# Two plain blocks ahead of the first feed-forward stage's doubles in an encoder layer on one NeuronCore, one double more, and another order of the operand combinations

## The chip, the cores and the metric

The kernel runs on one core of one Trainium2 chip. The metric is the time of one execution of the program on the device, in microseconds (us). A time given for a kernel is the median of its runs.

## What is computed

One layer of a bidirectional encoder with 512 tokens, 1024 features and float32 numbers. It adds half a SwiGLU feed-forward stage to x, then a mixer (a dilated local attention A, a grouped-query attention B with rotary embeddings, gates, an output projection), then half a second feed-forward stage, and normalises the result:

```python
def swiglu(x, w1, w3, w2):
    return (jax.nn.silu(x @ w1) * (x @ w3)) @ w2
...
    for l in range(DEPTH):
        x = x + 0.5 * swiglu(rmsnorm(x, ffn1_norm[l]), ffn1_w1[l], ffn1_w3[l], ffn1_w2[l])
        h = rmsnorm(x, mix_norm[l])
        x = x + hybrid_mixer(h, w_in[l], b_gate[l], q_norm[l], k_norm[l], rel_bias,
                             w_branch_a[l], w_branch_b[l], w_out[l], cos, sin)
        x = x + 0.5 * swiglu(rmsnorm(x, ffn2_norm[l]), ffn2_w1[l], ffn2_w3[l], ffn2_w2[l])
    return rmsnorm(x, final_norm)
```

`w1` and `w3` are 1024 x 2816, `w2` is 2816 x 1024. The hidden width of 2816 is 22 blocks of 128, numbered f = 0 to 21.

## The kernel before

**Arithmetic.** Each float32 operand is split into a high part that TensorE multiplies in one pass and the remainder (`H`, `L`). A product is three matmuls (`mm3`): H by H, H by L, L by H. For weights the split is a cast on ScalarE (`L234`, 128x1024) and a subtraction on VectorE (`L235`).

**Plain blocks.** The activations h lie as eight tiles of 128 features x 512 tokens (`hH0` to `hH7`, `hL0` to `hL7`). A plain block f takes one weight chunk of `w1` and one of `w3` (128x1024 each). Each chunk makes 8 steps of three matmuls with 512 columns in a PSUM bank of its own. The first block does both chunks together (`pair`), the others one after the other (`feat`). The loop over the plain blocks counts these steps: n = 0 to 63 with four blocks. After a step it calls hooks: at n = 12 the squares for the norm, at 23 the statistic (`stat_r`), at 28 its spreading over the partitions (`stat_R`, which gives `R`, the reciprocal norm of each token). The bank of a chunk can't be emptied before `R` is there, so these evictions are held and then issued at once (`done1`: a multiplication by `R`, `L473`, and a Silu; `done3`: `L477`). There are four such banks (`psm`, bufs=4): with four chunks held, the next product needs the bank of the first.

**Doubles.** From there on two blocks f, f+1 are done together by a seven-product scheme of Strassen's kind (`strassen`): steps A11, S1, S2, A12, S3, S4, A22, each of 8 x 3 matmuls with 256 columns. Steps S2 and S4 use weight sums that VectorE adds (`L233`). For S1 and S3 the sums are made by DMA: one load from SP's queue, and a second that adds to it from GpSimd's queue (`L215`, `L216`). The steps of following doubles are woven into each other (`slots`): A11, S1, S2, A12, then A11 of the next double, S3, S1 of the next, and so on.

**Operand combinations.** The doubles need combinations of the quarters of h. `t_steps` makes them: eight copies of the scaled x into two scratch tiles T0 and T1 (ScalarE, `L343`), four combinations on VectorE (`L356`, `L357`), and the splits of them: `part(0)` for S1, `part(3)` for S2, `part(2)` for A22 (`L348`, `L349`), and four small ones, `part1`, for S3 (`L353`, `L354`). The plain loop calls one of the first fifteen at n = 16, 18, ..., 44; the four small ones are called after the first steps of the doubles.

**What sets the order of the work.** TensorE's program order is the order of the code (`manual_schedule`). A scheduler orders the instructions of ScalarE, VectorE, GpSimd and SP's queue when the program is built; on the chip each of them runs its own list in that order. Weight chunks are used in the order of `self.order`; loads are issued in the order of `turn_of`, which puts the two-part sums (`wt`) four places earlier; every kind of buffer is a ring (`BUFS`): three raw chunks `wr`, three `wa`, two `ws`, four `wt`, and three split chunks `wh`/`wl` and one more, `whx`, which takes every fourth chunk.

**Groups.** `GROUPS` says at which f the plain blocks end and where the groups end, whose outputs go through `w2` together. In the first stage ("a") blocks 0 to 3 are plain, and 4 to 7 are two doubles; then `w2` for blocks 0 to 7, and two more groups of doubles. In the second ("b") blocks 0 and 1 are plain and 2 to 7 are three doubles.

Of the kernel before, what the change touches and what calls it, by code (L numbers as in the profile page):

```python
# [18 lines left out]
BUFS = {"wr": 3, "wa": 3, "ws": 2, "wt": 4, "wh": 3, "whx": 1}  # L19
BASE = {"wh": 160, "whx": 32}  # L20
EARLY, EARLIER = 4, 6
GROUPS = {"a": (4, 8, 16, 22), "b": (2, 8, 16, 22)}
PAIRS = ((0, 0), (1, 0), (0, 1), (0, 2), (1, 1), (1, 2), (2, 0), (3, 0), (2, 1), (2, 2), (3, 1), (3, 2))
NSQ = 10
STEPS = ("A11", "S1", "S2", "A12", "S3", "S4", "A22")
# [9 lines left out]
T = 512  # L35
# [34 lines left out]
class Layer:  # L70
    def __init__(self, ctx, tc, a):
        self.tc, self.nc, self.a = tc, tc.nc, a
        ctx.enter_context(tc.manual_schedule(engines={mybir.EngineType.PE}))
        pool = lambda n, **k: ctx.enter_context(tc.tile_pool(name=n, **k))
# [38 lines left out]
        self.raws, self.tiles, self.used, self.wx, self.TQ = {}, [], 0, None, None  # L113
# [46 lines left out]
    def ring(self, tag, n, done, last):  # L160
        held, bufs = self.rings[tag], BUFS[tag]
        pool = self.wb if tag in ("wr", "wh") else self.wx
        if pool is None or (len(held) >= bufs and held[-bufs] >= done):
            return None
        held.append(last)
        if tag[:2] != "wh":
            return pool.tile([128, 1024], F32, tag=tag, name=tag, bufs=bufs)
        at = (self.offset(n) - BASE[tag]) % 256 // 4
        return tuple(pool.tile([128, 1088], F32R, tag=t, name=t, bufs=bufs)[:, at:at + 1024] for t in ("wh", "wl"))
# [164 lines left out]
    def t_steps(self, g, gp):  # L334
        nc = self.nc
        raw, both = [], []
        flat = lambda t, c: t[:, c].rearrange("p k n -> p (k n)")

        def put(d):
            if d == 0:  # L340
                both.extend(gp.tile([128, 2048], F32, tag=f"g{2 + c}", name=f"T{c}") for c in range(2))
                raw.extend(both[c // 2][:, 1024 * (c % 2):1024 * (c % 2) + 1024] for c in range(4))
            nc.scalar.activation(both[d // 4].rearrange("p (a c) -> p a c", a=2)[:, :, 256 * (d % 4):256 * (d % 4) + 256],  # L343
                                 self.x[d].rearrange("p (a n) -> p a n", a=2), AF.Copy, scale=self.par[:, g + d:g + d + 1])

        def part(c):
            src, H, L = raw[c], flat(self.TH, max(0, c - 1)), flat(self.TL, max(0, c - 1))
            nc.scalar.copy(H, src)  # L348
            nc.vector.tensor_sub(L, src, f32(H))  # L349

        def part1(k):
            src, H, L = raw[1][:, 256 * k:256 * k + 256], self.hH[k][:, 256:512], self.hL[k][:, 256:512]
            nc.scalar.copy(H, src)  # L353
            nc.vector.tensor_sub(L, src, f32(H))  # L354

        sub = lambda o, a, b: nc.vector.tensor_sub(raw[o], raw[a], raw[b])  # L356
        neg = lambda o, a, b: nc.vector.scalar_tensor_tensor(raw[o], raw[a], -1.0, raw[b], op0=ALU.mult, op1=ALU.subtract)  # L357
        return ([lambda d=d: put(d) for d in range(NK)]
                + [lambda: sub(0, 0, 1), lambda: sub(1, 3, 1), lambda: neg(3, 3, 0), lambda: part(0),
                   lambda: neg(2, 3, 2), lambda: part(3), lambda: part(2)], [lambda k=k: part1(k) for k in range(4)])  # L360

    def block(self, name, n):
        if n % 8 == 0:
# [71 lines left out]
    def ffn(self, s, gin, gnext, hooks, out=None, side=None):  # L435
        with ExitStack() as ctx:
            pool = lambda n, **k: ctx.enter_context(self.tc.tile_pool(name=n, reuse_waits="tile", **k))
            tp = pool("hT", bufs=1, side="right")
            self.TH = tp.tile([128, 3, 4, 256], F32R, name="TH")
            self.TL = tp.tile([128, 3, 4, 256], F32R, name="TL")  # L440
            self.wx = self.shifted(pool("wx", bufs=1), 128)
            self.cp = self.shifted(pool("c", bufs=2), 128)
            self.ffn_run(s, gin, gnext, hooks, out, side or {}, pool("g", bufs=1))
            self.wx = None

    def ffn_run(self, s, gin, gnext, hooks, out, side, gp):
# [83 lines left out]

        first, *ends = GROUPS[s]

# [206 lines left out]
    def project_qk(self):  # L739
        nc, tc = self.nc, self.tc  # L740
        with ExitStack() as ctx:
            pool = lambda n, **k: ctx.enter_context(tc.tile_pool(name=n, reuse_waits="tile", **k))
            tp = self.shifted(pool("qT", bufs=1), 64)
            self.TQ = [tp.tile([128, 4, 4, 256], F32R, name=f"TQ{c}") for c in "HL"]
            self.wx = self.shifted(pool("wxq", bufs=1), 64)
# [440 lines left out]
    def layer(self, out):  # L1186
# [7 lines left out]
        for d in range(NK):  # L1194
            nc.sync.dma_start(self.x[d], self.a["x"][d])
            if d % 2 == 0:
                s = slice(128 * d, 128 * d + 256)
# [121 lines left out]
```

## Time and profile before

| | |
|---|---|
| time before, median of 3 runs | 1253.38 us (1253.02 to 1253.86) |
| the profiled execution's own time | 1252.48 us |
| its span, first to last instruction | 1250.7 us |
| mean granted TensorE clock | 0.998 |
| TensorE busy | 1239.0 us, 99% of the span |
| VectorE busy | 891.4 us, 71% |
| ScalarE busy | 595.6 us, 48% |
| moved by DMA | 183.49 MB, mean 147 GB/s |

The profile is of one execution. Times in its timeline are microseconds from the start of the span. PE is TensorE, DVE is VectorE, ACT is ScalarE, POOL is GpSimd; SPq and POOLq are the queues that issue DMAs. A row of the timeline gives start, duration, engine, line, operation, output<-input, shapes and, in brackets, how long the engine sat idle before it and what ended that. Durations of matmuls overlap (they are pipelined), so a matmul's price is the distance from its start to the next one's start. On DVE and ACT, too, an operation starts a little before the one ahead of it has ended.

### The profile page before, as it was taken

The page shows a single profiled execution, that of the slowest core. Times are in us where ns is not written, and L with a number is a line of the kernel's source. Part 1 is how long each engine was busy: PE and PEld are TensorE (multiplying, and loading weights), DVE is VectorE, ACT ScalarE, POOL GpSimd, SP SyncE. Part 2 cuts the span into 40 slices and gives each one's busy share as a digit, 9 for nine tenths or more (in the row PEclk, how much of TensorE's full clock was granted, in tenths as well). Part 3 has the DMA queues.
Part 4 walks back from the last instruction along what each step waited for, and adds up shares of the span by engine and source line. Part 5 has one row for each costly group of instructions (what it writes and reads, how often), then busy time and mean ns, then how long its engine had stood idle before and what let it go on. Part 6 is the DMA issues. An engine that isn't in the chain of part 4 may idle for free.

```text
span 1250.7 us, 20135 instructions
## 1 busy us (share of the span) xinstructions
PE 1239.0 (99%) x8076; PEld 1112.9 (89%) x8076; DVE 891.4 (71%) x1344; ACT 595.6 (48%) x886; POOL 122.6 (10%) x128
## 2 busy tenths in 40 slices
PE   9999999999999999999999999999999999999997
PEld 7897999899898999978888878888889989988997
DVE  7784688468784887567745898866678747874874
ACT  8551365245463444454423546654475425532553
POOL 1111101000210210200000200000301001100001
PEclk9999999999999999999999999999999999999999
DMA  9875777241486882762242220157737536743222
GB/s 299 229 193 166 194 194 197 87 119 55 148 209 190 226 236 87 228 186 78 84 141 88 81 93 18 34 155 233 218 101 189 166 101 185 187 151 107 63 85 68
DMA packets 85981, 183.49 MB, mean 147 GB/s; under 512 B 12528, under 2 KB 19072, under 8 KB 85888
## 3 DMA queue, kind: packets, MB, share of 16 engines
q1 hardware_dynamic: 68048, 141.27, 33.7%
q0 software_dynamic: 17120, 40.39, 16.1%
q8 instruction: 63, 1.03, 0.3%
q10 hardware_dynamic: 720, 0.55, 0.1%
q14 instruction: 30, 0.25, 0.1%
HBM read 170.55 MB, written 15.29 MB: 149 GB/s over the span
## 4 chain that ended last, share of the span: by engine, by line
PE 97%; DVE 1%; ACT 1%; DMA 0%; issue 0%; SPq 0%; POOL 0%; DVEq 0%
PE mm L249 25%; PE mm L251 24%; PE mm L250 24%; PE Y L250 4%; PE Y L249 4%; PE Y L251 4%; PE X L250 2%; PE X L251 2%; PE X L249 2%; PE mm L937 1%; PE S L861 1%; PE Tb L1073 1%; PE T L948 1%; PE Sb L251 1%; PE Sb L250 1%; PE Sb L249 1%
## 5 line engine op out<-in xcount | busy, mean ns | idle before, releaser
L234 ACT CAST wh<-wr 128x1024 fp32r<-128x1024 f32 x139 | 145.9, 1049 | 194.7 <-PE mm L250 125.7
L235 DVE TENSOR_TENSOR wl<-wr,wh 128x1024 fp32r<-128x1024 f32 x139 | 169.6, 1221 | 51.5 <-ACT wh L234 51.2
L249 PE MATMUL mm<-hH,wh 128*128 128x256 f32 (+1 forms) x600 | 198.2, 330 | 0.0
L251 PE MATMUL mm<-hH,wl 128*128 128x256 f32 (+1 forms) x600 | 195.4, 326 | 1.0 <-DVE wl L235 1.0
L250 PE MATMUL mm<-hL,wh 128*128 128x256 f32 (+1 forms) x600 | 195.5, 326 | 0.3 <-DVE hL L389 0.3
L249 PE MATMUL mm<-gg,wh 128*128 128x512 f32 (+1 forms) x376 | 141.5, 376 | 0.0
L250 PE MATMUL mm<-gg,wh 128*128 128x512 f32 (+1 forms) x376 | 141.0, 375 | 0.0
L251 PE MATMUL mm<-gg,wl 128*128 128x512 f32 (+1 forms) x376 | 141.0, 375 | 0.0
L251 PEld LDWEIGHTS mm<-hH,wl 128*128 128x128 f32 x600 | 112.9, 188 | 11.8 <-DVE wl L235 1.4
L249 PEld LDWEIGHTS mm<-hH,wh 128*128 128x128 f32 x600 | 112.8, 188 | 11.7 <-issue 1.0
L250 PEld LDWEIGHTS mm<-hL,wh 128*128 128x128 f32 x600 | 113.0, 188 | 10.4 <-DVE hL L389 0.8
L234 ACT CAST wh<-wa 128x1024 fp32r<-128x1024 f32 x50 | 52.6, 1052 | 102.1 <-PE mm L250 55.4
L234 ACT CAST wh<-wt 128x1024 fp32r<-128x1024 f32 x50 | 52.6, 1052 | 71.1 <-PE mm L250 46.4
L235 DVE TENSOR_TENSOR wl<-wt,wh 128x1024 fp32r<-128x1024 f32 x50 | 61.2, 1224 | 33.1 <-ACT wh L234 32.4
L234 ACT CAST wh<-ws 128x1024 fp32r<-128x1024 f32 x50 | 52.6, 1052 | 66.6 <-PE mm L250 47.5
L249 PE MATMUL mm<-TH,wh 128*128 128x256 f32 x304 | 83.9, 276 | 0.0
L250 PE MATMUL mm<-TL,wh 128*128 128x256 f32 x304 | 83.9, 276 | 0.0
L251 PE MATMUL mm<-TH,wl 128*128 128x256 f32 x304 | 83.9, 276 | 0.0
L249 PEld LDWEIGHTS mm<-gg,wh 128*128 128x128 f32 x376 | 70.6, 188 | 14.1 <-PE mm L251 0.9
L251 PEld LDWEIGHTS mm<-gg,wl 128*128 128x128 f32 x376 | 70.6, 188 | 12.9
L250 PEld LDWEIGHTS mm<-gg,wh 128*128 128x128 f32 x376 | 70.6, 188 | 12.6
L545 DVE TENSOR_TENSOR u<-mm,R 128x512 f32<-128x512 f32 x40 | 27.7, 691 | 75.7 <-PE mm L251 75.5
(270 smaller groups left out, 3210.0 us busy)
## 6 DMA issues: line engine op xcount, KB each, us to landing
wr<-in_w2a SPq DMA_DIRECT2D x22, 512.0 KB, 3.4
wr<-in_w2b SPq DMA_DIRECT2D x22, 512.0 KB, 3.5
wt<-in_w13b SPq DMA_DIRECT2D x20, 512.0 KB, 3.5
wa<-in_w13b SPq DMA_DIRECT2D x20, 512.0 KB, 3.3
wt<-in_w13b POOLq DMA_DIRECT2D x20, 512.0 KB, 6.0
wt<-in_w13a SPq DMA_DIRECT2D x18, 512.0 KB, 3.5
wt<-in_w13a POOLq DMA_DIRECT2D x18, 512.0 KB, 6.1
wa<-in_w13a SPq DMA_DIRECT2D x18, 512.0 KB, 3.4
```

The source lines that it names most:

```text
L234: self.nc.scalar.copy(H, raw)
L235: self.nc.vector.tensor_sub(L, raw, f32(H))
L249: mm(out, lH, rH, start=start, stop=False, skip_group_check=more)
L250: mm(out, lH, rL, start=False, stop=False, skip_group_check=more)
L251: mm(out, lL, rH, start=False, stop=stop, skip_group_check=more)
L545: nc.vector.tensor_mul(u, ps, R)
L861: nc.tensor.matmul(*args, start=True, stop=True)
L937: nc.tensor.matmul(oc, v, p, start=st, stop=sp)
L948: nc.tensor.transpose(ps[:, 128 * b:128 * b + 128], P[h][:, c0 + 128 * b:c0 + 128 * b + 128], self.ident)
L1073: nc.tensor.transpose(pt[:, 128 * j:128 * j + 128], P[h, j][:, 128 * k:128 * k + 128], self.ident)
```

## The change

Five edits. `GROUPS["a"]` starts with 2 instead of 4: blocks 2 and 3, which were plain, become a double. The hooks of the first stage move: squares from n = 12 to 10, `stat_r` from 23 to 22, `stat_R` from 28 to 27, and the combinations from every second step from n = 16 to every step from n = 15. `t_steps` returns another list, for both feed-forward stages: `part(0)` directly behind the combination that it needs, `part(3)` next, and the combination and split for A22 (`neg(2,3,2)`, `part(2)`) moved behind the four small splits, to the calls after the first steps of the doubles. The ring gives out a buffer for a double's weights (other than split ones) only to the stage that runs.

```diff
-GROUPS = {"a": (4, 8, 16, 22), "b": (2, 8, 16, 22)}
+GROUPS = {"a": (2, 8, 16, 22), "b": (2, 8, 16, 22)}
...
-        if pool is None or (len(held) >= bufs and held[-bufs] >= done):
+        s = self.order[n][0]
+        if pool is None or s[:2] == "sw" and tag != "wh" and s[2] != self.stage or (len(held) >= bufs and held[-bufs] >= done):
             return None
...
         return ([lambda d=d: put(d) for d in range(NK)]
-                + [lambda: sub(0, 0, 1), lambda: sub(1, 3, 1), lambda: neg(3, 3, 0), lambda: part(0),
-                   lambda: neg(2, 3, 2), lambda: part(3), lambda: part(2)], [lambda k=k: part1(k) for k in range(4)])
+                + [lambda: sub(0, 0, 1), lambda: part(0), lambda: sub(1, 3, 1), lambda: neg(3, 3, 0), lambda: part(3)],
+                [lambda k=k: part1(k) for k in range(4)] + [lambda: neg(2, 3, 2), lambda: part(2)])
...
-            hooks = {12: squares, 23: self.stat_r, 28: self.stat_R, "T": (16, 2)}
+            hooks = {10: squares, 22: self.stat_r, 27: self.stat_R, "T": (15, 1)}
```

In the changed kernel all line numbers from 160 on are one higher. The scheduler orders the other engines anew; three places are shown here. In the rows `acc<-acc,sq` sums the squares, `wl` is the remainder of a weight chunk (`wl<-wr,wh` of a plain one), `ws` a weight sum, `ms` the first step from the statistic to `R`, T_316 and T_317 are T0 and T1 (T_302 and T_303 in the changed kernel), `TL` the remainder of a combination, `t_381` (`t_377`) the eviction of the first chunk's bank.

VectorE from the last sums of squares on, which is where TensorE starts the second plain block; before:

```order
L399 TENSOR_TENSOR acc<-acc,sq 128x512 x3
L235 TENSOR_TENSOR wl<-wr,wh 128x1024
L399 TENSOR_TENSOR acc<-acc,sq 128x512
L356 TENSOR_TENSOR T_316<-T_316 128x1024
L235 TENSOR_TENSOR wl<-wr,wh 128x1024 x2
L356 TENSOR_TENSOR T_316<-T_317,T_316 128x1024
```

The same place in the changed kernel:

```order
L400 TENSOR_TENSOR acc<-acc,sq 128x512 x4
L357 TENSOR_TENSOR T_302<-T_302 128x1024
L236 TENSOR_TENSOR wl<-wr,wh 128x1024 x2
L234 TENSOR_TENSOR ws<-wt,wa 128x1024
L236 TENSOR_TENSOR wl<-wa,wh 128x1024
L357 TENSOR_TENSOR T_302<-T_303,T_302 128x1024
```

The remainder of the second block's first chunk, which stood ahead of the last sum of squares, stands behind it and behind the first combination now; and a weight sum `ws<-wt,wa` stands between.

VectorE from the statistic to the first eviction; before:

```order
L405 TENSOR_SCALAR ms<-stat 128x4
L357 SCALAR_TENSOR_TENSOR T_317<-T_317,T_316 128x1024
L235 TENSOR_TENSOR wl<-wr,wh 128x1024
L349 TENSOR_TENSOR TL<-T_316,TH 128x1024
L357 SCALAR_TENSOR_TENSOR T_317<-T_317 128x1024
L473 TENSOR_TENSOR t_381<-mm,R 128x512
```

The same place in the changed kernel, from the operation behind `ms<-stat` and the first `TL` on:

```order
L358 SCALAR_TENSOR_TENSOR T_303<-T_303,T_302 128x1024
L236 TENSOR_TENSOR wl<-wt,wh 128x1024
L236 TENSOR_TENSOR wl<-wa,wh 128x1024
L350 TENSOR_TENSOR TL<-T_303,TH 128x1024
L355 TENSOR_TENSOR hL_105<-T_302,hH_97 128x256
L355 TENSOR_TENSOR hL_106<-T_302,hH_98 128x256
L355 TENSOR_TENSOR hL_107<-T_302,hH_99 128x256
L355 TENSOR_TENSOR hL_108<-T_302,hH_100 128x256
L358 SCALAR_TENSOR_TENSOR T_303<-T_303 128x1024
L234 TENSOR_TENSOR ws<-ws,wa 128x1024
L350 TENSOR_TENSOR TL<-T_303,TH 128x1024
L474 TENSOR_TENSOR t_377<-mm,R 128x512
```

Between the statistic and the first eviction stood four operations of 1024 columns; now there are eight of them (the first `TL` is not in the rows) and four of 256.

ScalarE from the last square on, at the second plain block; before:

```order
L397 ACTIVATE sq<-x_81 128x512
L234 CAST wh<-wr 128x1024
L343 ACTIVATE T_316<-x_75,par 128x2x256
L343 ACTIVATE T_316<-x_76,par 128x2x256
L343 ACTIVATE T_316<-x_77,par 128x2x256
L343 ACTIVATE T_317<-x_78,par 128x2x256
L234 CAST wh<-wr 128x1024
```

And in the changed kernel:

```order
L398 ACTIVATE sq<-x_81 128x512
L344 ACTIVATE T_302<-x_75,par 128x2x256
L344 ACTIVATE T_302<-x_76,par 128x2x256
L344 ACTIVATE T_302<-x_77,par 128x2x256
L235 CAST wh<-wr 128x1024
L344 ACTIVATE T_303<-x_78,par 128x2x256
L235 CAST wh<-wr 128x1024
```

Three copies of x into T0 stand ahead of the cast of the second block's first chunk now.

On GpSimd's list one adding load stood ahead of the operation that finishes the statistic (`r<-ms`), and three stand there now; on SP's list the first `wt` load stands one place earlier, ahead of the second block's first chunk.

More of the change, by code (lines that the diff above doesn't have):

```diff
@@ L112, in __init__ @@
         self.order += self.ffn_order("b")
-        self.raws, self.tiles, self.used, self.wx, self.TQ = {}, [], 0, None, None
+        self.raws, self.tiles, self.used, self.wx, self.TQ, self.stage = {}, [], 0, None, None, None
         self.cap = len(self.order)
@@ L440, in ffn @@
             self.TL = tp.tile([128, 3, 4, 256], F32R, name="TL")
-            self.wx = self.shifted(pool("wx", bufs=1), 128)
+            self.wx, self.stage = self.shifted(pool("wx", bufs=1), 128), s
             self.cp = self.shifted(pool("c", bufs=2), 128)
@@ L744, in project_qk @@
             self.TQ = [tp.tile([128, 4, 4, 256], F32R, name=f"TQ{c}") for c in "HL"]
-            self.wx = self.shifted(pool("wxq", bufs=1), 64)
+            self.wx, self.stage = self.shifted(pool("wxq", bufs=1), 64), "q"
             cp, qp = pool("cq", bufs=2), pool("qo", bufs=2)
```

## Prediction

> **What bounds the kernel now.** I read the page's busy times first, then the list of who waited for whom on TensorE, then TensorE's timeline over the first 92 us, where the change lies.
>
> ```profile
> PE 1239.0 (99%) x8076; PEld 1112.9 (89%) x8076; DVE 891.4 (71%) x1344; ACT 595.6 (48%) x886; POOL 122.6 (10%) x128
> ```
>
> TensorE works 1239.0 of 1250.7 us. So the time is the sum of TensorE's matmuls plus its waits, and these are few:
>
> ```profile
> PE warm L1193 <- POOL R L94: 1.3, 1, 1.3
> PE rb L422 <- POOL r L406: 1.0, 1, 1.0
> PE mm L251 <- DVE wl L235: 1.0, 1, 1.0
> ```
>
> They are the longest of the whole run: the first at the start, the second in the last stage, the third at the second plain block. A change can shorten this kernel by giving TensorE fewer columns, and lengthen it by a wait. Here are TensorE's marks:
>
> ```profile
> 17.88 0.39 PE L250 MATMUL mm<-hL,wh 128*128 128x512 f32 x1
> 19.29 0.50 PE L251 MATMUL mm<-hH,wl 128*128 128x512 f32 x1 [1.02 <-DVE wl L235]
> 19.62 0.40 PE L249 MATMUL mm<-hH,wh 128*128 128x512 f32 x1
> 19.86 0.39 PE L250 MATMUL mm<-hL,wh 128*128 128x512 f32 x1
> ...
> 24.41 0.95 PE L413 MATMUL stat<-ones,acc 128*128 128x1 f32 x8
> ...
> 31.21 0.39 PE L249 MATMUL mm<-hH,wh 128*128 128x512 f32 x1
> ...
> 52.97 0.28 PE L249 MATMUL mm<-hH,wh 128*128 128x256 f32 x1
> ...
> 91.17 0.39 PE L249 MATMUL mm<-gg,wh 128*128 128x512 f32 x1
> ```
>
> 19.29 is the third matmul of step n = 16, held for the remainder of its weights. 24.41 is the statistic. 31.21 is step n = 32, the start of plain blocks 2 and 3; it takes over the bank of the very first chunk. 52.97 starts the two doubles, 91.17 the product with `w2`.
>
> **The change part by part.**
>
> *Columns.* Blocks 2 and 3 as plain ones take 52.97 - 31.21 = 21.76 us. Two doubles take 91.17 - 52.97 = 38.20, one 19.10. The order has 72 matmuls more (7 x 24 - 4 x 24), at half the columns. Gain: 2.66 us.
>
> *The second block's first chunk.* These are the rows of VectorE and then of ScalarE around it, and on to the first evictions:
>
> ```profile
> 15.82 2.28 DVE L399 TENSOR_TENSOR acc<-acc,sq 128x512 f32<-128x512 f32 x3
> 18.02 1.22 DVE L235 TENSOR_TENSOR wl<-wr,wh 128x1024 fp32r<-128x1024 f32 x1
> 19.15 0.69 DVE L399 TENSOR_TENSOR acc<-acc,sq 128x512 f32<-128x512 f32 x1
> 19.75 1.22 DVE L356 TENSOR_TENSOR T<-T 128x1024 f32<-128x1024 f32 x1
> ...
> 25.39 0.16 DVE L405 TENSOR_SCALAR ms<-stat 128x4 f32<-128x4 f32 x1 [0.43 <-PE stat L413]
> 25.47 1.22 DVE L357 SCALAR_TENSOR_TENSOR T<-T,T 128x1024 f32<-128x1024 f32 x1
> 26.60 1.22 DVE L235 TENSOR_TENSOR wl<-wr,wh 128x1024 fp32r<-128x1024 f32 x1
> ...
> 30.02 1.29 DVE L473 TENSOR_TENSOR t<-mm,R 128x512 f32<-128x512 f32 x2
> ...
> 49.78 1.54 DVE L354 TENSOR_TENSOR hL<-T,hH 128x256 fp32r<-128x256 f32 x4
> ```
>
> ```profile
> 16.46 1.03 ACT L234 CAST wh<-wr 128x1024 fp32r<-128x1024 f32 x1
> 17.40 2.56 ACT L343 ACTIVATE T<-x,par 128x512 f32<-128x512 f32 x4
> 19.87 1.03 ACT L234 CAST wh<-wr 128x1024 fp32r<-128x1024 f32 x1
> ```
>
> VectorE is at work without a gap at 18.02; an operation of 1024 columns holds it 1.14 us (four of them lie between 25.47 and 30.02), one sum of squares 0.60 (19.15 to 19.75). In the new order the remainder stands behind the fourth sum and the first combination: it starts at 18.02 + 0.60 + 1.14 = 19.76 and ends 1.22 later at 20.98; before it ended at 19.24 and TensorE went on at 19.29. So TensorE goes on at 21.03, 1.74 us later. ScalarE doesn't add to it: three copies at (19.87 - 17.40) / 4 = 0.62 and the cast of 1.03 from 16.46 on end at 19.35. Nothing else hides it: the first block's matmuls end where they did. Cost: 1.74 us.
>
> *The first double's bank.* The first step A11 stands where step n = 32 stood: 31.21 + 1.74 = 32.95. Like n = 32 it needs the bank of the first chunk, which `L473` empties. Before, this eviction starts at 30.02, and one operation of 512 columns takes 0.69, so the first bank was free near 30.7, half a us ahead of 31.21. What now stands on VectorE ahead of it? The statistic comes one step of three matmuls earlier in the code (21.76 us for 32 steps, 0.68 each), so at 24.41 - 0.68 + 1.74 = 25.47; `ms` follows 0.98 behind (25.39 - 24.41), at 26.45. Behind `ms` (0.08) come eight operations of 1024 columns and four of 256: 8 x 1.14 + 1.54 = 10.66. So `L473` starts at 37.19 and ends at 37.88, and A11 starts at 37.9 at the soonest. The operations wait for little in between: casts on ScalarE and four releases of h by TensorE, which end before 31 us by the same sum. Wait: 37.9 - 32.95 = 4.95 us.
>
> Behind the waiting A11 all of TensorE's list is queued; nothing overtakes it. The first chunk's bank is the one that matters: the next three come free with the next three evictions while A11 runs.
>
> *The adding loads.* Ahead of `ms` VectorE now has three more operations, the first of which, the weight sum `ws<-wt,wa`, needs the first adding load landed:
>
> ```profile
> L216 POOL DMA_DIRECT2D wt<-in_w13a x5: 1195/1204/1365, 17.0 to 54.9; - x5
> ...
> DMA to landing us min/median/max: 5.6/9.0/11.6
> ```
>
> ```profile
> 10.39 0.42 SPq L201 DMA_DIRECT2D wr<-in_w13a  x1
> ```
>
> ```profile
> wr<-in_w13a SPq DMA_DIRECT2D x1, 512.0 KB, 5.0
> ```
>
> The `wt` load takes the place of the load at 10.39, which landed 5.0 us later, so GpSimd issues the addition at about 15.4. VectorE needs it by 26.45 - 3 x 1.14 = 23.0, that is within 7.6 us. The shortest of the five flights is 5.6, the median 9.0, the longest 11.6: from 2.0 us early to 4.0 late. The new one is the first, with no other addition ahead of it, but it has the doubles' loads beside it; I take 8.3, a little below the median. Cost: 0.7 us, bounds 0 and 4.0. The other two additions stand ahead of `r<-ms` on GpSimd, but `R` is wanted on VectorE only at 37, so some us there are covered by the chain above.
>
> *What costs nothing.* The third double's loads, casts and evictions have the pace of the two before it, which ran from 52.97 to 91.17 without a wait of TensorE. The new order of the combinations in the second feed-forward stage moves a combination and a split behind the eviction; TensorE didn't wait there, so nothing is gained, and if the cover failed the price were one operation, 1.2. Later stages take another of the four split buffers at each chunk, since the count is three chunks higher; bounds 0.5 either way, half of a wait such as the list shows. The ring's new condition only withholds loads whose stage isn't open.
>
> *A clock rule.* TensorE's first matmuls are slow:
>
> ```profile
> 4.85 0.80 PE L249 MATMUL mm<-hH,wh 128*128 128x512 f32 x1
> ...
> 7.17 0.39 PE L251 MATMUL mm<-hH,wl 128*128 128x512 f32 x1
> 7.40 0.47 PE L249 MATMUL mm<-hH,wh 128*128 128x512 f32 x1
> ```
>
> The six from 4.85 to 7.40 take 2.55 us, 0.43 each, against 0.23 later (7.17 to 7.40). Behind the wait of 1.02 us they are 0.33 and 0.24 apart, nearly at pace. So a cold TensorE would cost 2.55 - 6 x 0.23 = 1.2 us, and a short wait doesn't make it cold; I take nothing. The Trainium skill, "TensorE: Matmul & The Clock Gate", Part 1, says that an idle window of about 3.4 us puts TensorE's clock to half speed until it has been busy for such a window. The start and the short wait agree with that, and no wait of some 5 us is in the trace. By that rule the sum could have 1.7 us more, an estimate from the page's window.
>
> *The sum.* -2.66 + 1.74 + 4.95 + 0.7 = +4.7 us on the profiled execution's 1252.48 (span 1250.7 and 1.8 around it), 1257.2. The median lies 0.9 above that execution, so 1258.1.
>
> **The rivals.**
>
> *The eviction is not what A11 waits for, or VectorE gets there in time.* Then only the second block's wait is new: -2.66 + 1.74 = -0.9, 1252.5, no change; without that wait too 1250.7, just faster. It decides if `L473` ends before 32.95, which needs some 5 us less on VectorE's list than the order shows. For it: VectorE is busy only 71% over the run. Against: from 18 to 31 us it hardly rests, by its rows, and the new list is longer there. 1252.5 gets 0.10, 1250.7 gets 0.05.
>
> *TensorE restarts cold.* If the wait of some 5 us brings back the pace of the start, 0.43 instead of 0.23, for as long as there, it costs the 1.2 us from above: 1259.3. The clock rule above is this case. For it: the slow start. Against: the pace behind the short wait. 0.22.
>
> *The additions land late.* With 11.6 us instead of 8.3 everything behind `ws<-wt,wa` is 3.3 later: 1261.4. For it: additions beside a full queue take 9 and more in the trace. Against: the first has no addition ahead of it. 0.13.
>
> That the change doesn't do what it says is excluded: the order shows the matmuls of one double more.
>
> **How the numbers follow.** My forecast, 1258.1, gets the remaining 0.50. From a measurement of this kernel 0.2%, 2.5 us, can be told from no change: below 1250.9 is faster, above 1255.9 slower. Faster 0.05 and same 0.10 are the first rival, slower 0.85 the rest. The range: the forecast's own bounds are 1257.4 without the 0.7, less 1.2 for my reading of starts and ends and 0.5 for the later stages, 1255.7; upwards the cold case and the late one but for its last 0.2, 1261.2. That leaves out the first rival and the far end of the third.
>
> **What would show it.** Right: TensorE has a wait of near 2.8 us at the third matmul of n = 16 for `wl`, and one of about 5 at the first 256-column matmul, released by VectorE's `t<-mm,R`; VectorE has no gap over 0.5 us from `ms` to it; the doubles then take 57.3 us without a wait. Wrong: A11 starts before 34 us, the wait ends on another engine, or the three doubles show new waits. If matmuls behind the wait lie 0.2 apart instead of 0.11, the cold case holds. If `ws<-wt,wa` starts past 23, the additions cost what I gave them or more.

## The result, and the profile after

The changed kernel takes 1263.17 us in the median of 6 runs (1262.36 to 1265.25); the kernel before 1253.2 in 6 runs beside them (1252.54 to 1253.86). The ratio is 1.0081, with an interval of 1.0071 to 1.0092. So it is slower, as forecast, but by 10.0 us where the forecast had 4.7, and outside the forecast's range. The profiled execution of the changed kernel is the slowest of its six: 1265.25 us, with a span of 1263.4.

The page's busy times, granted clock by slices, and chain of work that ended last:

```profile
PE 1241.0 (98%) x8148; PEld 1117.3 (88%) x8148; DVE 901.3 (71%) x1350; ACT 599.1 (47%) x890; POOL 125.9 (10%) x130
...
PEclk9899999999999999999999999999999999999999
...
PE 93%; DVE 4%; DMA 2%; issue 0%; POOL 0%; ACT 0%; SPq 0%; DVEq 0%; POOLq 0%; ACTq 0%
```

There are 72 matmuls more, as the order said. The chain, which before ran 97% over TensorE, now spends 4% on VectorE and 2% on a DMA. The second slice (31.6 to 63.2 us) has a lower granted clock than any slice of the kernel before. Who waited for whom on TensorE:

```profile
PE mm L250 <- DVE t L474: 4.0, 1, 4.0
PE rb L423 <- POOL r L407: 4.0, 2, 2.9
PE mm L250 <- ACT wh L235: 1.7, 1, 1.7
PE T L949 <- DVE MX L870: 1.4, 2, 1.2
PE warm L1194 <- POOL R L94: 1.3, 1, 1.3
```

The first row is the wait that the forecast named: A11 for VectorE's eviction of the first chunk's bank. TensorE's marks:

```profile
19.43 0.50 PE L250 MATMUL mm<-hH,wh 128*128 128x512 f32 x1 [1.73 <-ACT wh L235]
21.28 0.50 PE L252 MATMUL mm<-hH,wl 128*128 128x512 f32 x1 [1.11 <-DVE wl L236]
...
25.74 0.50 PE L414 MATMUL stat<-ones,acc 128*128 128x1 f32 x4
...
33.14 0.96 PE L423 MATMUL rb<-ident,r 128*128 128x128 f32 x4 [2.94 <-POOL r L407]
...
42.20 0.58 PE L250 MATMUL mm<-hH,wh 128*128 128x256 f32 x1 [4.05 <-DVE t L474]
42.58 0.42 PE L251 MATMUL mm<-hL,wh 128*128 128x256 f32 x1
...
47.04 0.28 PE L251 MATMUL mm<-hL,wh 128*128 128x256 f32 x1
...
101.89 0.39 PE L250 MATMUL mm<-gg,wh 128*128 128x512 f32 x1
```

The third matmul of n = 16 lies 0.25 us and the statistic 0.27 us behind the forecast (21.03 and 25.47). A11 starts at 42.20 where the forecast's sum had 37.9 + 0.7 = 38.6. From 42.20 to 47.04 its matmuls lie some 0.2 us apart, twice their usual distance. The doubles take 101.89 - 42.20 = 59.69 us, not 57.3. VectorE between:

```profile
20.00 2.36 DVE L236 TENSOR_TENSOR wl<-wr,wh 128x1024 fp32r<-128x1024 f32 x2
27.49 1.23 DVE L234 TENSOR_TENSOR ws<-wt,wa 128x1024 f32<-128x1024 f32 x1 [5.13 <-DMA wt<-in_w13a]
...
30.90 0.16 DVE L406 TENSOR_SCALAR ms<-stat 128x4 f32<-128x4 f32 x1
...
41.46 1.28 DVE L474 TENSOR_TENSOR t<-mm,R 128x512 f32<-128x512 f32 x2
```

`ws<-wt,wa` waits 5.13 us for the first adding load; then there is no gap up to the eviction, 10.56 us behind `ms`. The late `ms` holds `r` too, and TensorE waits 2.94 us for it at `rb`, ahead of the 4.05 us at A11. TensorE's granted clock is the number ahead of the last two (DMA share, GB/s) in these windows of 2 us:

```profile
34.00:36.00 2.00, 2.00 (x6) 1.55 (x6) 2.00 (x3) 1.07 (x3) 0.00 (x0) 0.50 1.08 286
...
40.00:42.00 2.00, 0.00 (x0) 0.00 (x0) 2.00 (x3) 1.98 (x3) 0.94 (x1) 0.54 1.11 325
42.00:44.00 2.00, 1.80 (x8) 1.80 (x9) 1.90 (x4) 1.89 (x4) 0.27 (x1) 0.50 1.10 235
44.00:46.00 2.00, 2.00 (x12) 2.00 (x11) 1.76 (x3) 1.38 (x3) 0.00 (x0) 0.50 1.11 310
46.00:48.00 2.00, 2.00 (x15) 2.00 (x15) 1.94 (x3) 0.64 (x1) 0.00 (x0) 0.75 0.90 173
48.00:50.00 2.00, 2.00 (x20) 2.00 (x19) 1.22 (x1) 0.89 (x2) 0.00 (x0) 1.00 0.10 19
```

Half clock stands behind both long waits, that for `rb` and that before A11.

### The profile page after: what moved, and what is told of

It reads as the page before. It is cut to its first block, busy times and chain, and to the rows that moved or that the text cites. A ratio compares the mean times of both kernels' runs of the same rounds, so it can differ in the third digit from the quotient of the medians.

```text
span 1263.4 us, 20296 instructions
## 1 busy us (share of the span) xinstructions
PE 1241.0 (98%) x8148; PEld 1117.3 (88%) x8148; DVE 901.3 (71%) x1350; ACT 599.1 (47%) x890; POOL 125.9 (10%) x130
## 4 chain that ended last, share of the span: by engine, by line
PE 93%; DVE 4%; DMA 2%; issue 0%; POOL 0%; ACT 0%; SPq 0%; DVEq 0%; POOLq 0%; ACTq 0%
PE mm L250 23%; PE mm L252 23%; PE mm L251 23%; PE Y L252 4%; PE Y L250 4%; PE Y L251 4%; PE X L252 2%; PE X L250 2%; PE X L251 2%; DMA wt<-in_w13a 1%; PE S L862 1%; PE mm L938 1%; PE Tb L1074 1%; PE T L949 1%; DVE wl L236 1%; PE Sb L252 0%
## 5 line engine op out<-in xcount | busy, mean ns | idle before, releaser
L235 ACT CAST wh<-wr 128x1024 fp32r<-128x1024 f32 x136 | 142.6, 1049 | 193.0 <-PE mm L251 128.8
L250 PE MATMUL mm<-hH,wh 128*128 128x256 f32 (+1 forms) x584 | 191.9, 329 | 6.0 <-DVE t L474 4.0
L252 PE MATMUL mm<-hH,wl 128*128 128x256 f32 (+1 forms) x584 | 188.7, 323 | 1.1 <-DVE wl L236 1.1
L251 PE MATMUL mm<-hL,wh 128*128 128x256 f32 (+1 forms) x584 | 188.9, 323 | 0.3 <-DVE hL L390 0.3
L250 PE MATMUL mm<-TH,wh 128*128 128x256 f32 x320 | 88.4, 276 | 0.0
L251 PE MATMUL mm<-TL,wh 128*128 128x256 f32 x320 | 88.3, 276 | 0.0
L252 PE MATMUL mm<-TH,wl 128*128 128x256 f32 x320 | 88.3, 276 | 0.0
L236 DVE TENSOR_TENSOR wl<-wa,wh 128x1024 fp32r<-128x1024 f32 x52 | 63.5, 1221 | 26.1 <-ACT wh L235 26.1
```

The source lines that it names most:

```text
L235: self.nc.scalar.copy(H, raw)
L236: self.nc.vector.tensor_sub(L, raw, f32(H))
L250: mm(out, lH, rH, start=start, stop=False, skip_group_check=more)
L251: mm(out, lH, rL, start=False, stop=False, skip_group_check=more)
L252: mm(out, lL, rH, start=False, stop=stop, skip_group_check=more)
```

## The experiments

The theory at the outset: the price is VectorE's list ahead of the first eviction; it starts with `ms`, and `ms` came late because of the adding load. Rivals: the new order of the combinations costs by itself; the bank isn't the gate; the clock, not the list, is the price. "Before" in a ratio is the kernel before, run beside it on the same chip; w2 stands for the start of the first product with `w2` in the profiled execution (91.17 before, 101.89 in the changed kernel). The changed kernel's profiled execution is 2.1 us above its median, so a mark that is some 2 us earlier than in that profile need not show in a median.

**1. The new order of the combinations alone, in the kernel before.** The edit is the `t_steps` part of the change, nothing else.

> The kernel before with only the new order of the operand combinations, in both feed-forward stages; four plain blocks, hooks as before. If the loss comes from the double's earlier start on a full VectorE list (the list theory), there are 21.8 us more of plain work here and nothing waits: 1253.2, within 0.2%. If the new order itself costs (the order rival, for instance the combination for A22 coming too late in one of the two stages), it shows here: 1255 or more.

Measured: 1252.93 us (11 runs), ratio 1.0000 [0.9991, 1.0009]; w2 at 91.54. The order alone costs nothing.

**2. The first addition left out.**

```diff
-            nc.gpsimd.dma_start(dst, part("A22" if step == "S1" else "A11"), accum_op=ALU.add)
+            if n != 5:
+                nc.gpsimd.dma_start(dst, part("A22" if step == "S1" else "A11"), accum_op=ALU.add)
```

> The changed kernel without GpSimd's addition into the first S1's weights (the sum for that one step is left out, so that chunk holds one summand alone). The list theory: ws<-wt,wa on VectorE no longer waits till 27.5 us, ms comes right behind the statistic at 26.9, the first eviction ends near 38, A11 starts near 38.2 instead of 42.2; the wait for r before the spreading shrinks from 2.9 us to under 0.5. 4 us less, and up to 2 more if TensorE's slow matmuls behind A11 go: 1257 to 1259. If instead the other two additions on GpSimd's list hold up r (the GpSimd rival), the wait for r stays over 2 us and the time at 1261 to 1263.

Measured: 1262.23 us (5 runs), ratio 1.0071 [1.0059, 1.0084]: only 0.9 us under the changed kernel. A11 starts at 41.29, w2 at 100.16. Its VectorE, and TensorE at n = 16:

```profile
22.85 1.22 DVE L235 TENSOR_TENSOR ws<-wt,wa 128x1024 f32<-128x1024 f32 x1
...
29.98 0.16 DVE L407 TENSOR_SCALAR ms<-stat 128x4 f32<-128x4 f32 x1 [3.65 <-PE stat L415]
...
40.55 1.28 DVE L475 TENSOR_TENSOR t<-mm,R 128x512 f32<-128x512 f32 x2
```

```profile
21.85 0.80 PE L253 MATMUL mm<-hH,wl 128*128 128x512 f32 x1 [1.10 <-DVE wl L237]
22.44 0.63 PE L251 MATMUL mm<-hH,wh 128*128 128x512 f32 x1
22.86 0.63 PE L252 MATMUL mm<-hL,wh 128*128 128x512 f32 x1
```

The sum now stands in its place at 22.85, but `ms` then waits 3.65 us for the statistic, because TensorE works 0.43 us apart, at half pace, behind the two waits of n = 16. The list behind `ms` is again 10.57 us long. A second cause took the place of the first.

**3. The two weight sums behind the eviction.** An added ordering constraint puts the `ws` additions on VectorE behind the first two evictions; n = 6 and 11, like the other n in the edits below, is a chunk's place in `self.order`.

```diff
+            with self.behind(n in (6, 11)):
+                self.nc.vector.tensor_add(raw, a, b)
...
+            self.evicted = nc.vector.tensor_mul(t[1], ps, self.R).ins
```

> The changed kernel with the two weight sums of the first double (S2's and S4's) queued on VectorE behind the first evictions; nothing else is told to move. The list theory: the wait for the addition no longer holds ms; one or two operations of 1.14 us fewer ahead of the eviction; wl of S1's weights still needs the addition (27.5, cast to 28.6). Eviction near 36.0, A11 near 36.5, wait of 3 to 3.5 us: 6 us less than the changed kernel, 1256 to 1258. The GpSimd rival: the wait for r stays, 1261 to 1263.

Measured: 1262.71 us (5 runs), ratio 1.0069 [1.0056, 1.0083]. `ms` at 28.72, held 2.17 us by the statistic (half pace behind n = 16 here too), eviction at 38.60, A11 at 39.34, w2 at 99.48. With the list 9.9 us long A11 follows it, as in run 2.

**4. The list behind the evictions.** Besides the sums, `part(3)`, `part(2)`, the four small splits, the `neg` combinations and the remainder of chunk n = 7 (A12's weights) go behind the first two evictions on VectorE.

> As the run before, and also the later combinations (neg, both splits behind part(0), the four small splits) and the split of A12's weights queued on VectorE behind the first evictions. The list theory: five operations of 1024 columns and the four small ones leave the list ahead of the eviction, it ends near 32, A11 starts near 33.3 without a wait over 0.5 us; the first double's later steps still find their operands (S2's weights near 37.6 for a step at 38.8). What is left is the gain of 2.7 and the 2.0 us at the second plain block: 1252.5 to 1253.5. If the first double is bound by the amount of VectorE's work and not by its order, the wait comes back at S2 or S3 as several us: 1256 or more.

Measured: 1255.64 us (11 runs, 1252.94 to 1257.54), ratio 1.0018 [1.0008, 1.0027]; `ms` at 26.39, then the eviction, behind a wait for ScalarE's copy of `R`, and A11 without a wait:

```profile
31.64 1.29 DVE L485 TENSOR_TENSOR t<-mm,R 128x512 f32<-128x512 f32 x2 [2.38 <-ACT R L436]
```

```profile
32.89 0.28 PE L256 MATMUL mm<-hH,wh 128*128 128x256 f32 x1
...
90.13 0.39 PE L256 MATMUL mm<-gg,wh 128*128 128x512 f32 x1
```

The profiled execution, 1253.08, is near the fastest of the eleven; the median is above what was expected, and no trace shows what the slower ones did. Taking operations out from ahead of the eviction takes away three quarters of the loss: the list and the bank are the gate.

**5. The first chunk's load in time as well.**

```diff
     def turn_of(self, n):
...
+        if n == 5:
+            return 2
```

> The kernel with the evictions first, and the first wt load one place later on SP's list, behind the second plain block's first chunk, as in the kernel before. The scheduler then puts that chunk's cast and remainder back ahead of the copies into T0. The list theory: the wait at the second plain block falls from 2.8 to 1.0 us, the addition lands some 0.5 us later, A11 waits under 1 us: 2.7 us less than the kernel before at best, 1250.5 to 1252. If the addition's later landing comes back at A11 in full, 1252.5 to 1253.5.

Measured: 1256.67 us (7 runs), ratio 1.0027 [1.0016, 1.0038]. The third matmul of n = 16 is at 19.27, as before the change: the 2 us there come from the place of the chunk's load, which the scheduler's list follows. But A11 waits 3.06 us, until 34.42, and w2 is at 93.50: S1's weights need the addition, which lands at 28.5 now, and their split stands ahead of the eviction on both engines. VectorE makes the remainder at 29.66 and then waits 1.65 us for `R`, which ScalarE copies at 33.06; its cast of these weights had waited 3.95 us for the addition.

**6. A bank of its own for A11.**

```diff
-                st[f, bank] = self.bank() if bank == "A" else self.aux(bank)
+                st[f, bank] = self.bank() if bank == "A" and (s, f) != ("a", 2) else self.aux(bank)
```

> The changed kernel with the first A11 in a PSUM bank of the other pool, so that it needs no eviction. If the bank is the gate, A11 starts as soon as the plain steps end, near 38.1 instead of 42.2; S2 then waits some 2 us for its split weights, which stand behind the evictions; 4 us and part of the slow matmuls less 2: 1258 to 1261. If A11 waited for its weights or for h, it stays at 42 and 1263.

Measured: 1263.03 us (4 runs), ratio 1.0082 [1.0067, 1.0097]. A11's and S2's first matmuls:

```profile
35.59 0.28 PE L250 MATMUL A<-hH,wh 128*128 128x256 f32 x1
...
46.08 0.58 PE L250 MATMUL A<-TH,wh 128*128 128x256 f32 x1 [4.77 <-ACT c L494]
```

A11 starts without a wait, so the bank was what it waited for. But S2 adds to A11's bank, and it waits 4.77 us until ScalarE has copied A11 out of it (`c<-A`, at 45.45); this copy stands behind `R` (39.41) and the Silus, which follow the same VectorE list. The gate moves two steps on; w2 is at 99.52, but the median is that of the changed kernel.

**7. Matmuls as filler ahead of A11 in the changed kernel.**

```diff
+        if s == "a":
+            fill = self.aux("fill")
+            for _ in range(16):
+                nc.tensor.matmul(fill, self.hH[5][:, :128], self.hH[4], start=True, stop=True)
```

> The changed kernel with 16 matmuls of 128x512 into an unused bank between the last plain step and A11 (work that the result doesn't need). If the idle time makes TensorE slow, A11 still starts at 42.2 but at full pace, 0.12 us apart instead of 0.21: 2.0 to 2.4 us less, 1261. If the slow pace has another reason (loads on the memory, the operands), the fillers change nothing or add: 1263 to 1265.

Measured: 1262.82 us (5 runs), ratio 1.0078 [1.0066, 1.0091]. A11 starts at 41.89 behind 2.02 us without work and at full pace, and the doubles take 99.22 - 41.89 = 57.33, the forecast's 57.3. The median is only 0.35 lower, so what the slow stretch costs in the executions without a trace isn't shown. The mean granted clock is 0.992 to 0.994 in all six executions of the changed kernel, 0.996 to 0.997 in four of the five here, and 0.996 to 0.998 in the kernel before beside the experiments; so all six had slow time, but this mean counts idle time too.

**8. The loads beside the addition held back** by small memsets, until the second block's split is done.

> The changed kernel with the six loads behind the first A11's (S3, S1, A12, A11, S3, A22) held until VectorE has split the second plain block's weights, at 22.3 us, by a memset of one column in each of their buffers. If the first addition is slow because of the loads beside it, it lands 6 to 7 us after its issue, near 23, instead of 11.2; ms follows the statistic, A11 starts near 38.5: 3.5 to 6 us less, 1257 to 1260. If an addition takes 11 us in any company here, nothing moves: 1263.

Measured: 1263.25 us (4 runs), ratio 1.0082 [1.0069, 1.0096]. The addition is issued at 15.66 and the sum starts at 23.84, 8.2 us later, where it took 11.2 beside the full queue (10.5 to 11.7 in the ten profiles in which these loads aren't held). So the loads beside it cost it about 3 us. `ms` still comes at 28.35, 1.0 behind its place in the list, held by the statistic, since n = 16 is at half pace again.

**9. All that hangs on the addition behind the evictions.**

> Edit: the kernel with the first chunk's load in time and the combinations behind the evictions, and now the first double's S1 operand too: its split's cast on ScalarE behind the copy of R, its remainder on VectorE behind the two evictions, and the combination neg(3,3,0) one step later, so that nothing that hangs on the first adding load stands ahead of the evictions on either engine. If VectorE's list and what it waits for ahead of the eviction are the whole price: third matmul of step n=16 at 19.3, statistic at about 24.7, R and the first eviction at about 30 without the 1.65 us that VectorE waited for R, A11 at 31.4 to 31.6 without a wait of over 0.3, the first w2 product at 88.7 to 89.5 (before 91.2), a time of 1250.5 to 1252.5, faster than before by 1 to 2.5 us; S1's remainder then comes at 34 to 35.5 and may cost up to 1 us there. If the three doubles cost in themselves more than two blocks and two doubles (loads, the ring of buffers, the sums), A11 starts as early but the w2 product comes at 91 or later and the time is 1253 or more.

Measured: 1260.33 us (6 runs), ratio 1.0050 [1.0038, 1.0062]. The marks are those of the second case, but not for its reason: A11 starts without a wait, and then its operands' order on VectorE and ScalarE makes S1 and S2 late one after the other:

```profile
35.49 0.39 PE L263 MATMUL Y<-TH,wl 128*128 128x256 f32 x1 [0.81 <-DVE wl L244]
40.28 0.39 PE L261 MATMUL mm<-TH,wh 128*128 128x256 f32 x1 [2.01 <-ACT wh L242]
42.07 0.58 PE L263 MATMUL mm<-TH,wl 128*128 128x256 f32 x1 [1.29 <-DVE wl L244]
```

w2 at 95.03. The list isn't only too long ahead of the eviction; it has to be in TensorE's order on both sides of it.

**10 and 11. The addition and the statistic apart, and together.** Run 10 is run 2 with the load's place of run 5; run 11 has that place alone.

> Edit: the changed kernel, the first adding load (first double's S1) left out, so that one operand lacks a part of its sum, and that sum's plain load issued behind the second block's first chunk instead of ahead of it. The list on VectorE stays ahead of the eviction. Theory that the addition and the statistic each take the other's place: with both out of the way the third matmul of n=16 is at 19.3 without the half clock behind it, ms at about 24.8, the eviction 11 to 12 us later at 36 to 37, A11 at 36.7 to 37.5 with a wait of 5 to 6 us and a slow start, the w2 product at 96 to 97.5, a time of 1258.5 to 1260.5: 2.7 to 4.7 us under the changed kernel, where leaving out the addition alone brought 0.9. Rival, that what is left is not the start of VectorE's list but something else at the start of the doubles: ms comes at 25, A11 still at 40 or later, time 1261.5 or more.

> Edit: the changed kernel, only the first sum's plain load issued behind the second block's first chunk. The addition is kept, and its landing at 28 to 29 then gates the remainder of the S1 operand on VectorE, which stands behind ms and ahead of the eviction. Theory that each takes the other's place: n=16 at 19.3, no slow stretch, statistic in time at about 24.7, but the list then stops for the addition; eviction at 38.5 to 40, A11 at 39.3 to 40.8, w2 product at 99 to 100.5, time 1261 to 1263, which is within 2 us of the changed kernel and 1.5 to 4 over the kernel without the addition. If the late statistic alone were the price, the time would be the same as without the addition, 1258.5 to 1260.5.

Measured: 1261.37 us (5 runs), ratio 1.0057 [1.0045, 1.0069], and 1266.46 us (4 runs), ratio 1.0102 [1.0087, 1.0116]. Both medians are higher than expected. In run 11 the sum `ws` stands ahead of `ms` and waits for the addition, where the expectation had only the remainder behind `ms` wait for it; so A11 starts at 43.55 and w2 at 102.36, 2.8 and 1.9 us behind the ends of what was expected. VectorE of run 10, then of run 11:

```profile
25.05 0.16 DVE L409 TENSOR_SCALAR ms<-stat 128x4 f32<-128x4 f32 x1 [0.31 <-PE stat L417]
...
36.77 1.28 DVE L477 TENSOR_TENSOR t<-mm,R 128x512 f32<-128x512 f32 x2
```

```profile
28.84 1.22 DVE L236 TENSOR_TENSOR ws<-wt,wa 128x1024 f32<-128x1024 f32 x1 [6.22 <-DMA wt<-in_w13a]
...
31.12 0.15 DVE L408 TENSOR_SCALAR ms<-stat 128x4 f32<-128x4 f32 x1
```

`ms` comes at 30.90 in the changed kernel, at 29.98 without the addition, at 31.12 with the load in time, and at 25.05 with both. Each cause alone holds it. With both gone A11 starts at 37.50 and w2 at 96.58, both as expected. The profiled time is higher than the marks want: from the mixer's statistic to that of the second feed-forward stage this execution takes 562.6 us, the changed kernel's 560.6, the kernel before 558.8. That stretch varies from execution to execution (558.8 to 563.5 over these profiles), mostly by waits of the attention's transposes `T` for VectorE.

**12 and 14. The lists in TensorE's order.** In run 12 VectorE has, behind the first two evictions, first the remainder for S1, then the sum for S2, then the other evictions; in run 14 ScalarE's casts for A12, S2 and the small operands stand behind its copy of `R` too.

```diff
                 if hooks[n] == self.stat_R:
+                    if s == "a":
...
+                        self.prep()
+                        self.prep()
+                        with self.behind():
...
+            with self.tc.issue_after(self.spread) if g == G_FFN1 and c else nullcontext():
+                nc.scalar.copy(H, src)
```

> Edit: the first chunk's load in time, the combinations behind the evictions, and behind these on VectorE first the remainder of the first double's S1 operand, then the sum for S2 (issued in the flush itself), and only then the other evictions, so that each operand of the first double is made in the order in which TensorE asks for it. If the whole price is the order of VectorE's list around the first eviction: n=16's third matmul at 19.4, R at 30 to 31, eviction at 30.7 to 31.7, A11 at 31.4 to 32.4, S1 and S2 each with a wait of under 0.5, no slow matmuls, the first w2 product at 88.7 to 90, and a time of 1251 to 1254, not over the kernel before and 9 to 12 us under the changed kernel. If the earlier start only moves the wait to the next operand, as it did with everything behind the evictions (waits of 0.8, 2.0 and 1.3 us and a slow stretch), the w2 product comes at 92 or later and the time is 1256 or more.

> Edit: the kernel with the evictions, S1's remainder and the sum for S2 in TensorE's order, and now ScalarE's list too: the casts of A12's weights, of the S2 operand and of the four small operands behind the copy of R (one of them waited for its load and kept R until 32.2 there). If R on ScalarE is what the last 1.5 us of A11's wait hung on: R at 29.3 to 30, eviction at 30 to 30.7, A11 at 31.4 to 32.0 without a wait, the first w2 product at 88.8 to 90.0 (before 91.2), time 1251.5 to 1253.5, faster than before by 0.5 to 2 us. If the casts that moved back are then late themselves, the wait reappears at S1 or S2 (over 0.5 us in the list of waits) and the time stays at 1254 or more.

Measured: 1254.07 us (11 runs), ratio 0.9999 [0.9991, 1.0008], and 1254.13 us (11 runs), ratio 0.9999 [0.9990, 1.0008]. In run 12 A11 waits 1.48 us for an `R` that a cast kept, and w2 is at 91.40. In run 14 `R`'s copy is at 29.00, and VectorE and TensorE go:

```profile
29.61 1.29 DVE L496 TENSOR_TENSOR t<-mm,R 128x512 f32<-128x512 f32 x2 [1.05 <-ACT R L447]
```

```profile
31.49 0.28 PE L265 MATMUL mm<-hH,wh 128*128 128x256 f32 x1
...
37.80 0.38 PE L265 MATMUL mm<-TH,wh 128*128 128x256 f32 x1 [0.59 <-ACT c L516]
...
89.69 0.39 PE L265 MATMUL mm<-gg,wh 128*128 128x512 f32 x1
```

A11 has no wait, S2 one of 0.59, and the product with `w2` starts 1.48 us earlier than before the change. Those marks are as expected but for S2: the copy `c` of A11's bank, for which it waits, stands on ScalarE behind three of the small casts that were moved back, and with 1254.13 us the time is that of the second case. The profiled execution, 1255.94, is the slowest of the eleven, and its list of waits tells a part:

```profile
PE T L985 <- DVE MX L906: 1.8, 4, 1.2
PE Tb L1110 <- DVE Pb L1104: 1.3, 1, 1.3
```

The wait of `Tb` is 0.2 in the kernel before and in run 1, and 1.2 to 1.3 in all the kernels with the third double, so about 1.0 of the gain is given back there; `T` varies. Both versions equal the kernel before, and neither beats it.

**13 and 15. Filler in the kernel without the addition** and with its load in time (run 10): 16 matmuls, then 24.

> Edit: the kernel without the first addition and with that sum's load behind the second block's first chunk, plus 16 matmuls of 128x512 whose result nothing uses, on TensorE ahead of A11, where it waited 5.8 us. If the wait itself makes TensorE slow afterwards (the clock theory): A11 still at 37.3 to 38, its matmuls 0.11 to 0.12 apart from the first on, the doubles in 57.2 to 57.6 instead of 59.1, the w2 product at 94.6 to 95.3, time 1.3 to 2 us under the kernel without the filler. If A11 is slow for another reason (its weights, its bank): the matmuls are 0.2 apart as before and the w2 product stays at 96.5; 16 matmuls of at least 0.22 us fill 3.5 us, so that nothing else moves.

> Edit: as the kernel without the first addition, with its load in time and with filler, but 24 filler matmuls of 0.23 us instead of 16, 5.4 us instead of 3.6, so that nearly the whole wait before A11 is filled (16 left 2.16 us idle, and A11 ran its first 1 us at full pace and then 3.4 us at half). If idle time of TensorE is what the clock answers to: A11 at 37.3 to 37.8 with a wait of under 0.6, all matmuls of the doubles 0.11 to 0.12 apart, granted clock 1.00 from 36 to 48, the doubles in 57.2 to 57.5, the w2 product at 94.6 to 95.1, 1.5 us under the two others. If the slow stretch has another cause (the long operand traffic there, the small matmuls), it stays 3 to 4 us long and the w2 product is at 96 or later.

Measured: 1259.06 us (5 runs), ratio 1.0041 [1.0027, 1.0054], and 1259.73 us (5 runs), ratio 1.0041 [1.0027, 1.0055]. With 16, TensorE still idles 2.16 us before A11; it starts at full pace and falls to half 0.9 us later:

```profile
37.46 0.39 PE L253 MATMUL mm<-hH,wh 128*128 128x256 f32 x1 [2.16 <-DVE t L477]
...
38.28 0.30 PE L253 MATMUL mm<-hH,wh 128*128 128x256 f32 x1
38.40 0.40 PE L254 MATMUL mm<-hL,wh 128*128 128x256 f32 x1
...
41.79 0.30 PE L255 MATMUL mm<-hH,wl 128*128 128x256 f32 x1
```

w2 is at 96.36, nearly that of run 10: the expectation for 16 failed. With 24 the idle time is 0.36 us, no stretch of the doubles is slow, and they take 95.14 - 37.80 = 57.34:

```profile
37.80 0.39 PE L253 MATMUL mm<-hH,wh 128*128 128x256 f32 x1 [0.36 <-DVE t L477]
...
95.14 0.39 PE L253 MATMUL mm<-gg,wh 128*128 128x512 f32 x1
```

Run 10's take 59.08. So idle time ahead of A11 is what the clock answers to, and 2 us can be enough. The two medians are the same to 0.1%, and the intervals of both ratios overlap run 10's, so the price in the time isn't settled by them; it is read from the marks, 1.7 us here and 2.4 in the changed kernel.

## Why the forecast was right in direction and wrong in size

The profiled executions differ by 1265.25 - 1252.48 = 12.8 us; the forecast had 4.7 between them.

**Columns, -2.66: right.** Where nothing waits inside, the three doubles take 57.33 (run 7) and 57.34 (run 15), against 57.3.

**The second block's first chunk, +1.74: right in size.** Measured 21.28 - 19.29 = 1.99. The one wait of 2.8 us that was forecast came as two, 1.73 for ScalarE's cast and 1.11 for the remainder.

**The first double's bank, +4.95: right in mechanism and length.** The gate (run 6), the list (run 4) and its length (10.56 behind `ms` against 10.66 + 0.08) are shown. With the addition out of the way and the statistic in time, A11 starts at 37.50 (run 10), 0.4 from the forecast's 37.9. That is luck in part: `ms` comes 1.4 us earlier there than forecast (25.05 against 26.45), and the list behind it is 1.0 us longer (11.72). The forecast left out ScalarE's list; the copy of `R` on it is what the eviction waits for in runs 4, 5, 9, 12 and 14.

**The adding loads, +0.7: this step failed.** "I take 8.3, a little below the median" came out as 11.2, from 16.25 instead of 15.4, by this row of GpSimd and the sum's row above:

```profile
16.25 1.36 POOL L217 DMA_DIRECT2D wt<-in_w13a  x1 [14.99 <-DMA wt<-in_w13a]
```

So the sum started at 27.49, not 23.7: 0.85 us of this is the issue, 2.9 the flight. Without the addition `ms` would have come 0.98 behind the statistic's 25.74, at 26.7; it came at 30.90. That is 4.2 us where the step gave 0.7, a little over its upper bound of 4.0. The reason given, that the first addition has none ahead of it, was the wrong one to weigh: 3 us of its flight are the loads beside it (run 8). In the trace of the kernel before the first addition, issued at 16.97, landed after 5.6 us, the shortest of the five; SP's queue issued four loads of 512 KB between 14.9 and 20.2 us there, and seven between 15.3 and 20.1 in the changed kernel. That the number of loads sets the flight fits both, but only run 8 varied it.

**The clock, 0: this step failed.** That "a short wait doesn't make it cold; I take nothing" was argued from a wait of 1.02 us, while the same sum forecast one of 4.95. In the changed kernel's profile the price was 59.69 - 57.33 = 2.4 us, twice the 1.2 of that rival, since the slow stretch lasts about 4.7 us (42.20 to 46.9) and not the 2.55 that the start showed. In the eight profiles with slow matmuls behind the wait before A11 the doubles take 58.81 to 60.14 us, so the price is 1.5 to 2.8. The Trainium skill, "TensorE: Matmul & The Clock Gate", Part 1, has half speed behind an idle window of some 3.4 us, with a window that runs freely. The estimate by that rule, 1.7, lies within the 1.5 to 2.8. The slow stretch of 3.4 us in run 13 (38.40 to 41.79) agrees with such a window; that its wait was only 2.16 us doesn't agree with the idle window as the page puts it. The changed kernel's 4.05 us are longer than that window, but its clock had fallen after some 2 us of them (a mean of 0.54 from 40 to 42 us, the last matmul at 37.75). Here the runs decide: about 2 us without work can be enough.

**Later stages, 0 with bounds of 0.5: too narrow.** The product with `w2` started 10.72 later, and the rest of the kernel took 2.0 us more, 1.0 of it at `Tb`, 0.7 at `T`, which varies from run to run.

**The sum of what was off:** 0.25 at n = 16, 3.5 for the addition, 2.4 for the clock, 2.0 later make 8.1, which is 12.8 - 4.7. This holds for the two profiled executions; the changed kernel's median is 2.1 us below its profiled one, and which of the terms is smaller there isn't shown.

**The rivals.** Two of them happened, the cold restart and the late addition, and they were priced as if only one could. The late addition lengthens the wait which makes the restart cold; together they give 1258.1 + 3.3 + 1.2 = 1262.6, near the 1263.17 measured. That it is so near is partly luck, since the clock's price in the profile was twice 1.2, and the 2.0 us of the later stages aren't in it. The range stopped at one of them. Also, nothing in the forecast said that if the addition were early, the statistic would be next: half pace behind the two waits of n = 16 held the statistic, and with it `ms`, until 29.98, 28.72 and 28.35 (runs 2, 3 and 8).

**What stays open.** It isn't shown why `Tb` waits 1.0 us more in every kernel with the third double, nor whether the shifted places of the split buffers cost anything in the later stages. It isn't shown either where the slow stretches stood in the executions without a trace, behind n = 16 or in A11, and what they cost there.

## What to carry to other kernels

When a step is brought forward, list what each engine has queued ahead of the release that it needs, and ask of each operation in it what it waits for: with several late inputs in one list, removing one only shows the next (A11 starts 0.9 us earlier without the addition alone, and 4.7 us earlier with the load in time as well). Rivals that feed each other belong in one sum, and the wait that you forecast is the one whose effect on the clock has to be priced. Fewer columns are won only if the lists of the engines beside stand in TensorE's order; here that brought the whole loss back, and no more.

## What the runs showed of the hardware

- TensorE went to half clock behind two waits of 1.6 to 2.0 and 1.0 to 1.2 us with two matmuls between them, in the profiles of runs 2, 3, 6, 7 and 8 (granted clock 0.50 to 0.55 from 22 to 24 us), and not in those of the changed kernel and run 4 (1.00 there), with waits of 1.73 and 1.11, and 1.89 and 0.97.
- Before A11 the idle times with no slow matmuls behind them were 0.36, 1.48 and 2.02 us (runs 15, 12 and 7); those with half clock were 2.16 (run 13), 3.06 (run 5), 3.95 (run 3), 4.05 (the changed kernel), and 4.60 to 5.79 (runs 2, 8, 10 and 11). After 2.16 the fall came 0.9 us after work had begun again; in the changed kernel it came while TensorE was idle, with a mean of 0.54 from 40 to 42 us and no matmul there.
- An adding load of 512 KB from GpSimd's queue, the first of its stage, took 5.6 us in the kernel before, 10.5 to 11.7 in ten profiles with the third double beside SP's full queue, and 8.2 with six of those loads held back; the median of all twenty in that stage is 5.8 by the changed kernel's page.
